# A two-layer encoder: the step sizes' projection in one block of 128 columns, and three transfers at other places

## The chip, the core and the metric

The kernel runs on one core of a Trainium2 chip. The metric is the device time of one execution in microseconds (us). The core has five engines that work through their own queues of instructions in order: TensorE (PE in the profile; PEld is its loading of weights), VectorE (DVE), ScalarE (ACT), GpSimd (POOL) and SyncE (SP, which here issues transfers only). They wait for each other through semaphores. Matmuls write to PSUM; everything else lies in SBUF or in the device's DRAM.

## The reference

512 tokens of 1024 channels go through two layers. Each layer is a token mixer and an ffn, each between two RMS norms and with a residual sum:

```
for layer in range(2):
    hn = rms_norm(x, norm_mix_pre[layer])
    m = retention_na_mixer(hn, ...) if layer == 0 else ssd_mixer(hn, ...)
    x = x + rms_norm(m, norm_mix_post[layer])
    f = conv_geglu_ffn(rms_norm(x, norm_ffn_pre[layer]), ...)
    x = x + rms_norm(f, norm_ffn_post[layer])
```

The change touches the second layer's mixer above all. It projects `hn` to gates z (2048 columns), inputs, B and C (3072), which go through a depthwise conv of width 5 and a silu, and raw step sizes (64 columns: 32 heads in two directions). From these come the step sizes and the decays of a chunked scan:

```
dt = softplus(dt_raw + dt_bias)
A = -exp(a_log)
log_a = dt * A
y = bidir_scan(C, B, x * dt[forward], x * dt[backward], log_a[forward], log_a[backward])
```

The scan works in chunks of 128 tokens: it needs cumulative sums of `log_a` in a chunk, and exponentials of these and of their differences to the chunk's total.

## The kernel before

**Precision.** Every fp32 product is made of three matmuls in a reduced fp32 type. A weight `w` is split by `split` (lines 84–87) into `hi`, a rounded copy (a CAST on ScalarE), and `lo`, what is left (a subtraction on VectorE); activations are split likewise into `xh` and `xl`. `mm3` adds hi·xh, lo·xh and hi·xl. In the profile these are lines L91, L92 and L93.

**Weights.** They come in units of 128 x 1024 (512 KB). `wunit` (lines 61–76) takes a tile `wst` (three buffers), issues the transfer on SyncE's queue, and splits it into `whi` and `wlo` (four buffers each) or into given tiles. A unit is one projection of 128 output columns: `proj_fm` runs 8 blocks of contraction x 3 matmuls of 512 tokens (24 matmuls), or in two token halves of 256 (48 smaller ones). The splits are given a priority of 60 over their place in the program, so that the scheduler may put them ahead.

**Order.** A scheduler takes the program's instructions in order of priority, with the tiles' buffers and dependencies as limits, and writes one fixed queue for each engine. An engine never passes an instruction that waits. `E.flush` runs the transposes of the last two token tiles (`LATE`), held back from the stage before so that projections may stand beside them.

**Start.** `trunk` issues the transfer of the first token tile, then that of the gain `g0` (a row broadcast to 128 partitions, 512 KB), then the other three token tiles, with the first weights between them. Each tile goes through `norm`: a sum of squares (ScalarE, Square, `sumsq` L128), a power -0.5 (GpSimd), a scaling `xs` (VectorE L139), transposes (TensorE L148) and the split into `xh` and `xl`. ScalarE loads a table of functions (ACT_TABLE_LOAD) where the function to come is not in the one loaded.

**Second mixer.** `mixer1` first projects three units (for the scan's `bf`, `cf` and the first `xf`) in two token halves: while the first half runs, the late token tiles are normed, transposed and split (lines 883–889). Then come the three convs: ScalarE opens each with scale and bias (L693), and VectorE adds four more taps (L696, two of 511 and two of 510 columns). Then `steps` (lines 597–665): the 64 columns of step sizes in 24 matmuls, `z` (L616), the softplus as a long chain on VectorE in `log1p_exp_neg` (L277 to L287, with one reciprocal), `dt`, `la`, the scan `pf` (L628), the totals `tot`, `et` and its diagonal matrix `diag` for a matmul `pe` that spreads the totals, the exponentials `ysc` and `sw`, a logarithm of `dt` (`lp_e`), and the transposes of `lp_e` and `sw` to tokens (`pt`, L664), copied to `tok`. Three more units for `xf` follow, their silus (L702, L705), and then the groups by an order written out by hand (`SLOTS`): the further projections `t6` to `t9` and those of the next group, the states, heads and pairs. The states need `sw`, the heads `lp_e` and `pf`.

**Mixer's end and last ffn.** The last group's output products run for each token tile with the two residual halves read back from `xd` (L869), each tile is normed, and the ffn (`ffn`, lines 223–270) starts with four units in token halves; the first two go to `whi` and `wlo`, the other two to tiles `hh` and `hl` of the ffn's own pool, which lies in memory that the mixer held.

Of the kernel before, what the change touches and what calls it, by code (L numbers as in the profile page):

```python
# [7 lines left out]
F32 = mybir.dt.float32  # L8
R32 = mybir.dt.float32r
BF16 = mybir.dt.bfloat16  # L10
U32 = mybir.dt.uint32
AF = mybir.ActivationFunctionType
ALU = mybir.AluOpType
# [13 lines left out]
class Env:  # L27
# [30 lines left out]
        self.xl = self.res.tile([P, KD, S], R32, name="xl")  # L58
        self.late, self.xs = [], {}

    def wunit(self, src, parts=None):


        nc = self.nc
        st = self.wst.tile([P, 1024], F32, name="wst")
        nc.sync.dma_start(st, src)
        halves = slice(0, 512), slice(512, 1024)
        if parts is None:
            hi, lo = self.whi.tile([P, 1024], R32, name="whi"), self.wlo.tile([P, 1024], R32, name="wlo")
            with self.tc.high_priority(60):  # L70
                self.split(hi, lo, st)
            return [(hi[:, c], lo[:, c]) for c in halves]
        with self.tc.high_priority(60):
            for j, c in enumerate(halves):
                self.split(parts[j], parts[j + 2], st[:, c])
        return [(parts[j], parts[j + 2]) for j in range(2)]

    def bcast(self, row):

        g = self.gain.tile([P, D], F32, name="gain")  # L80
        self.nc.sync.dma_start(g, row.partition_broadcast(P))
        return g

    def split(self, hi, lo, src):
# [135 lines left out]
    E.late += [lambda s=s: E.finish(s, st, done) for s in LATE]  # L220


def ffn(E, w_up, cw, w_down, g_post_row, done):

    nc, tc = E.nc, E.tc
    with ExitStack() as ctx:
        hp = ctx.enter_context(tc.tile_pool(name="ffn_h", bufs=NF))
        cp = ctx.enter_context(tc.tile_pool(name="ffn_c", bufs=1))
        cwt = cp.tile([P, 2, NF, 4], F32, name="cwt")
        nc.sync.dma_start(cwt, cw)  # L230
        hs = []

        def conv(ps, s, f):
            w = lambda i: cwt[:, s, f, i:i + 1]
            o = E.tmp.tile([P, S], F32, name=f"cv{s}", tag="tmp")
            nc.scalar.activation(o, ps, AF.Identity, scale=w(1), bias=w(3))  # L236
            nc.vector.scalar_tensor_tensor(o[:, 1:], ps[:, :S - 1], w(0), o[:, 1:], op0=ALU.mult, op1=ALU.add)  # L237
            nc.vector.scalar_tensor_tensor(o[:, :S - 1], ps[:, 1:], w(2), o[:, :S - 1], op0=ALU.mult, op1=ALU.add)  # L238
            return o

        def tail(f, pg, pv):
            g = conv(pg, 0, f)
            nc.scalar.activation(g, g, AF.Gelu_apprx_tanh)
            v = conv(pv, 1, f)
            nc.vector.tensor_tensor(v, g, v, op=ALU.mult)  # L245
            h = (hp.tile([P, S], R32, name="hh"), hp.tile([P, S], R32, name="hl"))
            E.split(*h, v)
            hs.append(h)

        extra = lambda i=0: [hp.tile([P, S], R32, name=n) for n in ("hh", "hh", "hl", "hl")]  # L250
        w0 = [[E.wunit(w_up[s, f], extra() if 2 * f + s >= 2 else None) for s in range(2)] for f in range(2)]
        p0 = [[E.mm.tile([P, S], F32, name="mm") for s in range(2)] for f in range(2)]
        for c in range(2):
            for i in range(4):
                f, s = i // 2, i % 2
                E.proj_fm(p0[f][s], w0[f][s], c * 256, c * 256 + 256)
                if c == 0 and i in (1, 2):
                    E.flush()
        for f in range(2):
            tail(f, *p0[f])  # L260
        for f in range(2, NF):
            ps = []
            for s in range(2):
                w = E.wunit(w_up[s, f])
                ps.append(E.mm.tile([P, S], F32, name="mm"))
                E.proj_fm(ps[-1], w)
            tail(f, *ps)
        g_post = E.bcast(g_post_row)
        batches = [[(0, u)] for u in (2, 2, 2, 2, 2, 1)] + [[(1, u)] for u in (2, 2, 1, 6)]
        down_tm(E, batches, w_down, lambda k: hs[k], g_post, done, lambda i: extra() if i not in (2, 3) else None)  # L270
# [289 lines left out]
TAIL = ("x0 s0", "x1 s1", "x2 s2 t0", "x3 s3 t1")  # L560


def mixer1(E, w_dt, w_fm, cw, dtc, cols, mask, w_out, g_post_row, done):

# [4 lines left out]
    with ExitStack() as ctx:  # L571
# [22 lines left out]
        pd = E.dram.tile([H2, S], F32, name="pd")  # L594
        yd = E.dram.tile([H2, S], F32, name="yd")

        def steps():

            st = E.wst.tile([P, 512], F32, name="wst")
            nc.sync.dma_start(st, w_dt)  # L600
            wh = E.whi.tile([P, 512], R32, name="whi")
            wl = E.wlo.tile([P, 512], R32, name="wlo")
            E.split(wh, wl, st)
            ps = E.mm.tile([P, S], F32, name="mm")
            for k in range(KD):
                c = slice(k * H2, k * H2 + H2)
                E.mm3(ps[:H2], wh[:, c], wl[:, c], E.xh[:, k], E.xl[:, k], k == 0, k == KD - 1)
            bc = few.tile([P, 3], F32, name="bc")
            nc.sync.dma_start(bc, dtc)
            nc.scalar.activation(bc[:, 1:2], bc[:, 1:2], AF.Exp)  # L610
# [4 lines left out]
            for i in range(2):  # L615
                nc.scalar.activation(z[i * H2:i * H2 + H2], ps[:H2, i * 256:i * 256 + 256], AF.Identity,  # L616
                                     bias=bc[:H2, 0:1])
            with tc.tile_pool(name="lp", bufs=1) as lpp:
                dt = lpp.tile([P, 256], F32, name="dt")
                sw = lpp.tile([P, 256], F32, name="sw")  # L620
# [227 lines left out]
        def out_mm(o, t, ws):  # L848
            ps = E.mm.tile([P, 512], F32, name="mm")
            tt = slice(t * P, (t + 1) * P)  # L850
            for k in range(4):
                yh, yl = o["y"][k]
                E.mm3(ps, yh[:, tt], yl[:, tt], *ws[k], k == 0, k == 3)
            return ps
# [26 lines left out]
            silus(o)  # L881

        w0 = [E.wunit(w_fm[0, i]) for i in range(3)]
        p0 = [E.mm.tile([P, S], F32, name="mm") for _ in range(3)]
        for c in range(2):
            for i, (w, ps) in enumerate(zip(w0, p0)):
                E.proj_fm(ps, w, c * 256, c * 256 + 256)
                if c == 0 and i > 0:
                    E.flush()
        for i in range(3):  # L890
            project(gs[0], i, p0[i])
        steps()
        three, ys, last = pool("m1e", 5), pool("m1y", 2), pool("m1f", 1)
        for _ in range(3):
            load(nc.sync)
# [32 lines left out]
        def fin(t, n, m):  # L928
# [2 lines left out]
        t4 = lambda pool, tags: [pool.tile([P, 512], R32, name="wo", tag=t) for t in tags]  # L931
        ws = [E.wunit(w_out[NG - 1, 0, 0]) + E.wunit(w_out[NG - 1, 0, 1]),
              E.wunit(w_out[NG - 1, 1, 0], t4(one, ("state00", "state10", "state01", "state11"))) + E.wunit(w_out[NG - 1, 1, 1], t4(four, ("yh", "yh", "yl", "yl")))]
        first = [out_mm(gs[-1], 0, ws[n]) for n in range(2)]
        rms(gs[-1])
        for t in range(NT):
# [6 lines left out]
def trunk(tc, x, norms, ab, ssd, ffns, out):  # L943

    nc = tc.nc
    with ExitStack() as ctx:
        E = Env(ctx, tc)
        w0 = []
        for t in range(NT):
            nc.sync.dma_start(E.x[:, t, :], x[t * P:(t + 1) * P])  # L950
            if t == 0:
                g0 = E.bcast(norms[0, 0])
            else:
                w0.append(E.wunit(ab[0][0, len(w0)]))
        for t in range(NT):
# [17 lines left out]

        mixer0(E, w0, *ab, norms[0, 1], then(norms[0, 2]))
        ffn(E, *ffns[0], norms[0, 3], then(norms[1, 0]))
        mixer1(E, *ssd, norms[1, 1], then(norms[1, 2]))
        ffn(E, *ffns[1], norms[1, 3], store)
        while E.late:
            E.flush()

# [106 lines left out]
```

## Time and profile before

| | us |
|---|---|
| three runs | 1420.84, 1422.07, 1422.39 (median 1422.07) |
| the profiled execution | 1422.91 |
| its span | 1421.1 |
| TensorE busy | 1395.8 (98%) |
| VectorE busy | 909.3 (64%) |
| ScalarE busy | 710.6 (50%) |
| GpSimd busy | 60.9 (4%) |

The profile is of one execution; its span is the time from the first to the last instruction, and 1.8 us lie around it. A matmul counts as busy from its start to its modelled end, and the next starts before that, so what a matmul costs in a row of matmuls is read from start to start. The clock granted to TensorE is given as a share of full speed (1.00 is 2.4 GHz, 0.50 is 1.2 GHz); on the page it is at 9 tenths or more in all forty slices.

### The profile page before, as it was taken

To read this page: it belongs to the slowest core of one execution; us is meant where nothing else is said; L and a number is where in the kernel's file an instruction comes from. 1 tells how busy PE (TensorE), PEld (TensorE's weight loads), DVE (VectorE), ACT (ScalarE), POOL (GpSimd) and SP (SyncE) were. 2 spreads that over 40 slices of the span, in tenths; PEclk is the share of its full clock that TensorE was granted. 3 is DMA by queue.
4 is the path that set the end of the run, shared out by engine and by line. 5 is a ranking of instruction groups with operands and counts; after the bars stand their busy time and mean duration, and the time that the engine had idled before them with its cause. 6 is when DMAs were issued, how large, how long until landed. Compare 5 with 4: busy or idle time off the path is not lost.

```text
span 1421.1 us, 17833 instructions
## 1 busy us (share of the span) xinstructions
PE 1395.8 (98%) x6838; PEld 1141.2 (80%) x6838; DVE 909.3 (64%) x1345; ACT 710.6 (50%) x1194; POOL 60.9 (4%) x66
## 2 busy tenths in 40 slices
PE   7999999999999999999999999999989999999998
PEld 6877777898888888888788788787878888888886
DVE  7368888765656652347878686997785665664232
ACT  5346666444444432324878787487344444443230
POOL 1010110100000000000000000010110000000000
PEclk9999999999999999999999999999999999999999
DMA  7443232233233322323566464363342233333231
GB/s 284 150 132 104 85 89 80 77 108 104 89 104 91 102 89 93 129 106 106 140 183 182 148 184 143 101 190 112 124 144 74 91 102 91 102 96 98 89 104 60
DMA packets 56437, 166.33 MB, mean 117 GB/s; under 512 B 6689, under 2 KB 7457, under 8 KB 56353
## 3 DMA queue, kind: packets, MB, share of 16 engines
q1 hardware_dynamic: 48464, 149.99, 33.2%
q10 hardware_dynamic: 7888, 15.21, 3.9%
q8 instruction: 54, 0.88, 0.3%
q14 instruction: 31, 0.25, 0.1%
HBM read 157.57 MB, written 5.51 MB: 115 GB/s over the span
## 4 chain that ended last, share of the span: by engine, by line
PE 89%; DVE 4%; ACT 3%; issue 2%; DMA 1%; POOL 0%; DVEq 0%; SPq 0%; POOLq 0%; ACTq 0%
PE mm L91 27%; PE mm L92 27%; PE mm L93 27%; PE pi L783 2%; PE py L803 1%; PE st L732 1%; PE y L459 1%; PE pt L148 1%; PE sc L443 1%; DVE wlo L87 1%; PE pt L676 0%; PE sc L444 0%; ACT whi L86 0%; DMA x<-in_x 0%; PE pt L511 0%
## 5 line engine op out<-in xcount | busy, mean ns | idle before, releaser
L91 PE MATMUL mm<-xh,whi 128*128 128x512 f32 (+1 forms) x1216 | 463.9, 382 | 0.4 <-ACT xh L86 0.2
L93 PE MATMUL mm<-xl,whi 128*128 128x512 f32 (+2 forms) x1216 | 463.3, 381 | 0.0
L92 PE MATMUL mm<-xh,wlo 128*128 128x512 f32 (+2 forms) x1216 | 462.1, 380 | 0.0
L87 DVE TENSOR_TENSOR wlo<-wst,whi 128x1024 fp32r<-128x1024 f32 (+1 forms) x208 | 254.8, 1226 | 135.0 <-ACT whi L86 131.7
L86 ACT CAST whi<-wst 128x1024 fp32r<-128x1024 f32 (+1 forms) x208 | 216.5, 1042 | 145.1 <-PE mm L92 123.4
L91 PEld LDWEIGHTS mm<-xh,whi 128*128 128x128 f32 x1216 | 228.3, 188 | 45.7 <-issue 2.3
L93 PEld LDWEIGHTS mm<-xl,whi 128*128 128x128 f32 (+1 forms) x1216 | 228.1, 188 | 44.1 <-issue 1.1
L92 PEld LDWEIGHTS mm<-xh,wlo 128*128 128x128 f32 (+1 forms) x1216 | 228.4, 188 | 42.4 <-issue 0.2
L237 DVE SCALAR_TENSOR_TENSOR cv<-mm,cwt,cv 128x511 f32<-128x511 f32 x88 | 66.0, 750 | 150.5 <-ACT cv L236 150.5
L236 ACT ACTIVATE cv<-mm,cwt 128x512 f32<-128x512 f32 x88 | 68.7, 780 | 128.0 <-PE mm L93 128.0
L91 PE MATMUL mm<-whi,hh 128*128 128x512 f32 x288 | 112.0, 389 | 0.0
L92 PE MATMUL mm<-whi,hl 128*128 128x512 f32 x288 | 112.0, 389 | 0.0
L93 PE MATMUL mm<-wlo,hh 128*128 128x512 f32 x288 | 112.0, 389 | 0.0
L762 ACT ACTIVATE pb<-pb,tok 128x128 f32<-128x128 f32 x256 | 81.3, 391 | 5.7 <-DMA pb<-pd 3.2
L86 ACT CAST hh<-cv 128x512 fp32r<-128x512 f32 x44 | 27.3, 621 | 103.3 <-DVE cv L245 103.3
L238 DVE SCALAR_TENSOR_TENSOR cv<-mm,cwt,cv 128x511 f32<-128x511 f32 x88 | 66.0, 750 | 3.0
L93 PEld LDWEIGHTS mm<-wlo,hh 128*128 128x128 f32 x288 | 54.1, 188 | 11.3
L91 PEld LDWEIGHTS mm<-whi,hh 128*128 128x128 f32 x288 | 54.1, 188 | 11.2
L92 PEld LDWEIGHTS mm<-whi,hl 128*128 128x128 f32 x288 | 54.1, 188 | 11.2
L696 DVE SCALAR_TENSOR_TENSOR xf<-mm,cwt,xf 128x511 f32<-128x511 f32 (+1 forms) x64 | 47.5, 744 | 8.1 <-ACT xf L693 7.8
L87 DVE TENSOR_TENSOR hl<-cv,hh 128x512 fp32r<-128x512 f32 x44 | 30.5, 693 | 28.9 <-ACT hh L86 28.9
L128 ACT ACTIVATE junk<-mm 128x512 bf16<-128x512 f32 x24 | 14.3, 596 | 68.7 <-PE mm L93 68.6
(250 smaller groups left out, 1877.1 us busy)
## 6 DMA issues: line engine op xcount, KB each, us to landing
wst<-in_f_up SPq DMA_DIRECT2D x88, 512.0 KB
wst<-in_f_down SPq DMA_DIRECT2D x44, 512.0 KB
wst<-in_c_fm SPq DMA_DIRECT2D x40, 512.0 KB
pb<-pd ACTq DMA_DIRECT2D x29, 512.0 KB
wst<-in_ab_fm SPq DMA_DIRECT2D x20, 512.0 KB
gain<-yd SPq DMA_DIRECT2D x32, 256.0 KB
wst<-in_c_out SPq DMA_DIRECT2D x16, 512.0 KB
gain<-in_norms SPq DMA_DIRECT2D x8, 512.0 KB
```

Of the source, the lines that this page charges most:

```text
L86: self.nc.scalar.copy(hi, src)
L87: self.nc.vector.tensor_tensor(lo, src, hi.bitcast(F32), op=ALU.subtract)
L91: mm(out, lh, rh, start=first, stop=False)
L92: mm(out, ll, rh, start=False, stop=False)
L93: mm(out, lh, rl, start=False, stop=last)
L128: self.nc.scalar.activation(self.junk[:, :w], src, AF.Square, scale=float(n) ** -0.5, accum_out=s)
L236: nc.scalar.activation(o, ps, AF.Identity, scale=w(1), bias=w(3))
L237: nc.vector.scalar_tensor_tensor(o[:, 1:], ps[:, :S - 1], w(0), o[:, 1:], op0=ALU.mult, op1=ALU.add)
L238: nc.vector.scalar_tensor_tensor(o[:, :S - 1], ps[:, 1:], w(2), o[:, :S - 1], op0=ALU.mult, op1=ALU.add)
L696: nc.vector.scalar_tensor_tensor(r[:, a], ps[:, b], wc(j), r[:, a], op0=ALU.mult, op1=ALU.add)
L762: nc.scalar.activation(pb[:, dr, c], pb[:, dr, c], AF.Identity, scale=1.0 - 2 * dr, bias=tok[:, 0, c, dr * H + h:dr * H + h + 1])
L783: nc.tensor.matmul(pi[:, c - 1 + dr], o["st"][dr, i][:, q * P:(q + 1) * P], o["t"][1][:, c * C:(c + 1) * C], start=True, stop=True)
```

## The change

1. **Steps' projection.** The weights' `hi` and `lo` parts stand side by side in one tile, for each of 8 blocks 64 + 64 columns. One matmul of 128 columns gives both parts' products in two halves of the partitions; with `xh` and `xl`, in two token halves of 256, these are 2 x 8 x 2 = 32 matmuls (`steps_proj`; the product lo·xl, left out before, is now in it). Two additions on VectorE join the parts into `z`. The projection and the whole chain behind it stand between the two token halves of the first three units, no longer behind their convs.
2. **Start.** The gain's transfer is issued by ScalarE. ScalarE runs one tiny Square of a constant before it waits for the first token tile, so that the table load belongs to that.
3. **Last ffn.** Its first two units and the transfer of the third are asked for within mixer1 (`ahead`), before the last group's first output products, and the transfer of the conv weights `cwt` after the four units.

```diff
+    def wload(self, src):
+        st = self.wst.tile([P, 1024], F32, name="wst")
+        self.nc.sync.dma_start(st, src)
+        return st
...
-    def bcast(self, row):
+    def bcast(self, row, eng=None):
         g = self.gain.tile([P, D], F32, name="gain")
-        self.nc.sync.dma_start(g, row.partition_broadcast(P))
+        (eng or self.nc.sync).dma_start(g, row.partition_broadcast(P))
...
-        nc.sync.dma_start(cwt, cw)
...
-        w0 = [[E.wunit(w_up[s, f], extra() if 2 * f + s >= 2 else None) for s in range(2)] for f in range(2)]
+        u0, u1, st = w1 or (E.wunit(w_up[0, 0]), E.wunit(w_up[1, 0]), None)
+        w0 = [[u0, u1], [E.wunit(w_up[0, 1], extra(), st), E.wunit(w_up[1, 1], extra())]]
+        nc.sync.dma_start(cwt, cw)
...
-        def steps():
+        def steps_weights():
             st = E.wst.tile([P, 512], F32, name="wst")
             nc.sync.dma_start(st, w_dt)
-            wh = E.whi.tile([P, 512], R32, name="whi")
-            wl = E.wlo.tile([P, 512], R32, name="wlo")
-            E.split(wh, wl, st)
-            ps = E.mm.tile([P, S], F32, name="mm")
+            w = E.whi.tile([P, KD, 2, H2], R32, name="whi")
+            with tc.high_priority(60):
+                E.split(w[:, :, 0], w[:, :, 1], st.rearrange("p (k h) -> p k h", k=KD))
+            return w.rearrange("p k a h -> p k (a h)")
+
+        def steps_proj(ps, w, c):
+            cc = slice(c * 256, c * 256 + 256)
             for k in range(KD):
-                c = slice(k * H2, k * H2 + H2)
-                E.mm3(ps[:H2], wh[:, c], wl[:, c], E.xh[:, k], E.xl[:, k], k == 0, k == KD - 1)
+                for j, x in enumerate((E.xh, E.xl)):
+                    nc.tensor.matmul(ps[:, cc], w[:, k], x[:, k, cc], start=k + j == 0, stop=k + j == KD)
+
+        def steps(ps):
...
+                nc.vector.tensor_tensor(z[i * H2:i * H2 + H2], ps[H2:, i * 256:i * 256 + 256], z[i * H2:i * H2 + H2], op=ALU.add)
...
-        p0 = [E.mm.tile([P, S], F32, name="mm") for _ in range(3)]
+        wd = steps_weights()
+        p0 = [E.mm.tile([P, S], F32, name="mm") for _ in range(4)]
         for c in range(2):
-            for i, (w, ps) in enumerate(zip(w0, p0)):
-                E.proj_fm(ps, w, c * 256, c * 256 + 256)
+            if c == 1:
+                steps_proj(p0[3], wd, 0)
+                steps_proj(p0[3], wd, 1)
+                steps(p0[3])
+            for i, w in enumerate(w0):
+                E.proj_fm(p0[i], w, c * 256, c * 256 + 256)
...
         for i in range(3):
             project(gs[0], i, p0[i])
-        steps()
...
+        ahead()
         first = [out_mm(gs[-1], 0, ws[n]) for n in range(2)]
...
-                g0 = E.bcast(norms[0, 0])
+                g0 = E.bcast(norms[0, 0], nc.scalar)
+                nc.scalar.activation(E.junk[:, :1], E.mhalf, AF.Square)
...
+        def ahead():
+            up = ffns[1][0]
+            w1.extend((E.wunit(up[0, 0]), E.wunit(up[1, 0]), E.wload(up[0, 1])))
```

Line numbers move with the change: the split is L86 and L87 before, L92 and L93 after; the convs' taps L696 before, L713 after.

**VectorE's order at mixer1's beginning.** The first piece is of before, with the splits of the fifth, sixth and seventh projections' weights (`wlo_5559`, `wlo_5596`, `wlo_5680`; the first three projections are those in token halves):

```order
L87 TENSOR_TENSOR wlo_5559<-wst_5556,whi_5558 128x1024
L696 SCALAR_TENSOR_TENSOR xf_5356<-mm_5171,cwt_5134,xf_5356 128x510
L277 SCALAR_TENSOR_TENSOR lp_e_5410<-z_5397 128x256
L87 TENSOR_TENSOR wlo_5596<-wst_5593,whi_5595 128x1024
L279 TENSOR_SCALAR lp_s_5411<-lp_e_5410 128x256
L87 TENSOR_TENSOR wlo_5680<-wst_5677,whi_5679 128x1024
L280 RECIPROCAL lp_s_5411<-lp_s_5411 128x256
L281 TENSOR_TENSOR lp_s_5411<-lp_s_5411,lp_e_5410 128x256
```

The second is of after, where `wlo_5690` is the seventh projection's:

```order
L713 SCALAR_TENSOR_TENSOR xf_5597<-mm_5572,cwt_5135,xf_5597 128x511
L642 TENSOR_SCALAR la_5316<-dt_5326,bc_5311 128x256
L643 MEMSET msk_5329 128x256
L675 TENSOR_SCALAR lp_e_5387<-dt_5326 128x256
L644 MEMSET msk_5329 128x2
L713 SCALAR_TENSOR_TENSOR xf_5597<-mm_5572,cwt_5135,xf_5597 128x510
L645 SCALAR_TENSOR_TENSOR pf_5317<-msk_5329,la_5316 128x256
L713 SCALAR_TENSOR_TENSOR xf_5597<-mm_5572,cwt_5135,xf_5597 128x510
L649 COPY tot_5361<-pf_5317 128x2
L93 TENSOR_TENSOR wlo_5690<-wst_5687,whi_5689 128x1024
L652 TENSOR_TENSOR pf_5317<-pf_5317,la_5316 32x256 x2
```

The seventh projection's split stood between the first operations of the softplus, ahead of the reciprocal and of all taps of the fourth projection's conv (`xf_5526` of before). Now it stands behind the whole softplus, the scan `pf`, the totals `tot` and the fifth projection's taps (`xf_5597` of after).

**ScalarE's order at the same place.** First before, from the table load for the logarithm on:

```order
L659 ACT_TABLE_LOAD
L659 ACTIVATE lp_e<-lp_e 128x256
L651 ACT_TABLE_LOAD
L651 ACTIVATE ysc<-pf 32x256
L638 ACTIVATE et<-tot 128x2
L651 ACTIVATE ysc<-pf 32x256
L86 CAST whi<-wst 128x1024
L654 ACTIVATE sw<-pf 32x256 x2
L652 ACTIVATE ysc<-tm 32x256
L653 ACTIVATE sw<-tm 32x256
L652 ACTIVATE ysc<-tm 32x256
```

And after, from the same load on (L668 to L671 are the exponentials, L722 a silu):

```order
L676 ACT_TABLE_LOAD
L676 ACTIVATE lp_e<-lp_e 128x256
L655 ACT_TABLE_LOAD
L655 ACTIVATE et<-tot 128x2
L668 ACTIVATE ysc<-pf 32x256 x2
L722 ACT_TABLE_LOAD
L722 ACTIVATE xf<-xf 128x512
L669 ACT_TABLE_LOAD
L669 ACTIVATE ysc<-tm 32x256
L663 COPY etot<-pe 128x2x2x64
L670 ACTIVATE sw<-tm 32x256
```

A silu of the first `xf` now stands between the exponentials, with a table load ahead of it and one behind it; a weights' cast that stood there has moved behind them, and `et` has moved ahead of the first `ysc`.

**SyncE's order around the last ffn.** First before (`wst<-in_f_up` is an up-projection unit's transfer, `x<-xd` the residual's):

```order
L66 DMA wst<-in_f_up 128x1024
L81 DMA gain<-in_norms 128x1024
L66 DMA wst<-in_f_up 128x1024 x2
L81 DMA gain<-in_norms 128x1024
L66 DMA wst<-in_f_up 128x1024 x2
L869 DMA x<-xd 128x512 x8
L66 DMA wst<-in_f_up 128x1024
```

And after:

```order
L64 DMA wst<-in_f_up 128x1024
L87 DMA gain<-in_norms 128x1024
L64 DMA wst<-in_f_up 128x1024 x2
L87 DMA gain<-in_norms 128x1024
L64 DMA wst<-in_f_up 128x1024 x2
L886 DMA x<-xd 128x512 x8
L64 DMA wst<-in_f_up 128x1024
```

The five up-projection transfers stand at the same places relative to the gains and to the residual's transfers, and the conv weights' transfer follows in both orders behind these rows.

At the start, ScalarE's queue of after begins with the gain's transfer, the table load and the tiny Square; then two sums of squares, the first weights' cast and the third sum of squares stand ahead of the first cast of `xh`, where before only two sums and the weights' cast stood ahead of it.

## Rows read from the trace of the kernel before

**Rows 1.** Windows: stretch, us, busy (instructions) of PE, PEld, DVE, ACT, POOL, clock, DMA share, GB/s.

```profile
0.00:14.00 14.00, 5.30 (x20) 4.05 (x20) 6.22 (x13) 8.07 (x12) 2.37 (x9) 1.00 0.88 322
...
660.00:690.00 30.00, 30.00 (x148) 24.19 (x147) 29.22 (x55) 17.33 (x23) 0.00 (x0) 1.00 0.27 88
690.00:712.00 22.00, 21.17 (x101) 14.99 (x100) 16.80 (x28) 20.04 (x49) 0.00 (x0) 1.00 0.82 206
712.00:1012.00 300.00, 299.04 (x1573) 242.41 (x1573) 240.03 (x354) 216.79 (x437) 18.53 (x13) 1.00 0.52 153
```

**Rows 2.** Waits of PE: what waited for what, us in total, times, longest.

```profile
PE pt L148 <- DVE xs L139: 9.1, 4, 8.2
PE mm L91 <- ACT hh L86: 3.9, 2, 3.2
```

**Rows 3.** Timeline of PE, mixer1's beginning: start us, us, instruction, [idle before it].

```profile
654.40 0.39 PE L91 MATMUL mm<-xh,whi 128*128 128x256 f32 x1 [0.24 <-ACT xh L86]
654.63 0.28 PE L92 MATMUL mm<-xh,wlo 128*128 128x256 f32 x1
654.75 0.29 PE L91 MATMUL mm<-xh,whi 128*128 128x256 f32 x1
...
663.35 0.39 PE L92 MATMUL mm<-xh,wlo 128*64 128x512 f32 x1
...
668.41 0.39 PE L93 MATMUL mm<-xl,whi 128*64 128x512 f32 x1
668.64 0.39 PE L91 MATMUL mm<-xh,whi 128*128 128x512 f32 x1
...
670.00 0.39 PE L91 MATMUL mm<-xh,whi 128*128 128x512 f32 x1
```

**Rows 4.** Timeline of DVE in mixer1, 668 to 700.

```profile
671.50 1.22 DVE L87 TENSOR_TENSOR wlo<-wst,whi 128x1024 fp32r<-128x1024 f32 x1
672.64 1.74 DVE L280 RECIPROCAL lp_s<-lp_s 128x256 f32<-128x256 f32 x1
...
677.61 0.41 DVE L285 TENSOR_TENSOR lp_r<-lp_r,lp_q 128x256 f32<-128x256 f32 x1
677.94 0.74 DVE L696 SCALAR_TENSOR_TENSOR xf<-mm,cwt,xf 128x510 f32<-128x510 f32 x1
678.60 0.28 DVE L286 TENSOR_SCALAR lp_r<-lp_r 128x256 f32<-128x256 f32 x1
678.80 1.22 DVE L87 TENSOR_TENSOR wlo<-wst,whi 128x1024 fp32r<-128x1024 f32 x1
679.94 0.42 DVE L285 TENSOR_TENSOR lp_r<-lp_r,lp_q 128x256 f32<-128x256 f32 x1
```

**Rows 5.** Timeline of ACT in mixer1, 655 to 700.

```profile
658.28 0.78 ACT L693 ACTIVATE bf<-mm,cwt 128x512 f32<-128x512 f32 x1 [3.44 <-PE mm L93]
...
681.64 0.61 ACT L705 ACTIVATE xf<-xf 128x512 f32<-128x512 f32 x1
...
688.62 1.28 ACT L651 ACT_TABLE_LOAD   x1
689.91 0.42 ACT L651 ACTIVATE ysc<-pf 32x256 f32<-32x256 f32 x1
```

**Rows 6.** Timeline of ACT at the start, 3 to 13.

```profile
4.25 1.28 ACT L128 ACT_TABLE_LOAD   x1 [4.25 <-DMA x<-in_x]
...
10.01 0.58 ACT L86 CAST xh<-pt 128x512 fp32r<-128x512 f32 x1
10.49 1.06 ACT L128 ACTIVATE junk<-x 128x1025 bf16<-128x1025 f32 x1
```

**Rows 7.** Timeline of PE at the start, 3 to 13.

```profile
11.24 0.77 PE L91 MATMUL mm<-whi,xh 128*128 128x512 f32 x1
```

**Rows 8.** Windows of 2 us at the last ffn's beginning, columns as in rows 1.

```profile
1056.00:1058.00 2.00, 1.54 (x5) 1.30 (x6) 2.00 (x4) 1.98 (x4) 0.00 (x0) 0.50 0.33 86
...
1062.00:1064.00 2.00, 2.00 (x17) 2.00 (x16) 0.43 (x1) 1.05 (x2) 0.00 (x0) 0.85 0.32 129
```

More of the change, by code (lines that the diff above doesn't have):

```diff
@@ L59, in __init__, with wunit @@
         self.late, self.xs = [], {}
-    def wunit(self, src, parts=None):
-        nc = self.nc
+    def wload(self, src):
         st = self.wst.tile([P, 1024], F32, name="wst")
-        nc.sync.dma_start(st, src)
+        self.nc.sync.dma_start(st, src)
+        return st
+    def wunit(self, src, parts=None, st=None):
+        if st is None:
+            st = self.wload(src)
         halves = slice(0, 512), slice(512, 1024)
@@ L220, in down_tm, with ffn @@
     E.late += [lambda s=s: E.finish(s, st, done) for s in LATE]
-def ffn(E, w_up, cw, w_down, g_post_row, done):
+def ffn(E, w_up, cw, w_down, g_post_row, done, w1=None):
     nc, tc = E.nc, E.tc
@@ L560, with mixer1 @@
 TAIL = ("x0 s0", "x1 s1", "x2 s2 t0", "x3 s3 t1")
-def mixer1(E, w_dt, w_fm, cw, dtc, cols, mask, w_out, g_post_row, done):
+def mixer1(E, w_dt, w_fm, cw, dtc, cols, mask, w_out, g_post_row, done, ahead):
     nc, tc = E.nc, E.tc
@@ L975, in trunk @@
         ffn(E, *ffns[0], norms[0, 3], then(norms[1, 0]))
-        mixer1(E, *ssd, norms[1, 1], then(norms[1, 2]))
-        ffn(E, *ffns[1], norms[1, 3], store)
+        w1 = []
+        def ahead():
+            up = ffns[1][0]
+            w1.extend((E.wunit(up[0, 0]), E.wunit(up[1, 0]), E.wload(up[0, 1])))
+        mixer1(E, *ssd, norms[1, 1], then(norms[1, 2]), ahead)
+        ffn(E, *ffns[1], norms[1, 3], store, w1)
         while E.late:
```

## Prediction

> **What bounds the kernel now.** I read the windows table first, then the waits of TensorE, then the timelines of the places that the change touches. The windows table shows TensorE busy in nearly all of every long stretch: 299.04 of 300 us in 712–1012, all 30 of 660–690 [rows 1]. So time can be gained or lost only where TensorE stops, where its matmuls cost something, and where its clock is low. The waits name two large stops: 9.1 us on the first `xs` (8.2 of them the start) and 3.9 us on the casts `hh` at the last ffn's beginning [rows 2]. In mixer1's beginning, where most of the change lies, TensorE hardly waits, but VectorE is nearly as full: 29.22 of 30 us in 660–690, and in 690–712 ScalarE is the fullest but one, with 20.04 of 22 [rows 1]. A change there is a matter of who is late, not of how much work there is.
>
> **Steps' matmuls.** Before, 24 products of 64 weight columns with 512 tokens; the run of 23 starts at 663.35, the last at 668.41, and the next projection at 668.64: 5.29 us, 0.23 each; one more stands alone among the earlier ones, 5.5 us in all [rows 3]. After, 2 halves x 8 blocks x 2 inputs = 32 products of 128 columns with 256 tokens. Such a product starts 0.12 after the one before it (654.63, 654.75) [rows 3], so 32 x 0.12 = 3.84. They stand ahead of the matmul at 654.40 that waited 0.24 for a cast of `xh` [rows 3], and cover that wait: counted from 654.16, they end at 658.0, the 72 second-half products of the first three projections (72 x 0.12 = 8.64) at 666.6, where before they and the steps ended at 668.6. **−2.0**. The two additions of the weight parts (64x256 on VectorE) have no row; the nearest are a 128x256 product at 0.33 start to start and a conv part of 511 columns at 0.66 [rows 4]. I take 0.4 each, between the two. They lie ahead of the conv parts, while VectorE waits for the first projection, and cost the path nothing as long as it does.
>
> **What the moved chain does to VectorE.** The orders of before and after decide this term. I number the projections of 512 columns by their place: the fourth starts at 668.64 before. Before, VectorE splits the fifth to seventh projections' weights (`wlo`) ahead of the reciprocal: the seventh's starts at 671.50, and TensorE needs it some 13 us later (668.64 + 3 x 24 x 0.227 = 685.0, with 0.227 from 668.64 to 670.00, six products) [rows 3, 4]. After, the chain of the step sizes begins ahead of the conv parts, and each of its links stands between two of them; the seventh's `wlo` stands behind the scan and the copy `tot`. Summing VectorE's list in the after order from the first conv part to the end of that `wlo`, start to start from [rows 4]: 20 conv parts x 0.66 = 13.2; 3 `wlo` x 1.14 = 3.4; the reciprocal 1.74; 10 two-input operations of 128x256 x 0.33 = 3.3; 10 with one input x 0.20 = 2.0; scan, memsets and copy about 1 (an estimate: the scan as two of those with one input, the others smaller). 24.6 us. The list can start when the first projection has ended (658.0 + 24 x 0.12 = 660.9) and ScalarE has opened its conv (0.78) [rows 5]: 661.7. The seventh's `wlo` ends at **686.3**.
>
> TensorE meanwhile: the fourth projection 666.6 to 672.1; the fifth's `wlo` ends at 672.7 by the same list, two products are put before it, a wait of 0.2; fifth and sixth end at 683.1. The order has three products with `whi` alone (seventh, eighth, ninth) before the first that reads the late `wlo`; these end at 683.8. Then TensorE stands until 686.3: **+2.5, with the small wait +2.7**. Bounds: nothing if VectorE's list is 10% shorter than summed, +4 if it loses a microsecond to links that wait for each other.
>
> **What it does to ScalarE.** Before, the loads of the function tables near there are Silu, Ln, Exp, all exponentials, Silu. After, a Silu load, one silu and another Exp load stand between the first exponentials and those that make `sw`. A load takes 1.28 (the activation behind it starts 1.29 later), an exponential 0.42, a silu 0.61 [rows 5]. By VectorE's list the fourth projection's convs end at 680.6; Silu load, three silus, Ln load, Ln, Exp load: 680.6 + 1.28 + 1.8 + 1.28 + 0.42 + 1.28 = 686.7, where `et` runs, not later than the `tot` that it needs. From there: two exponentials 0.84, Silu load 1.28, silu 0.61, Exp load 1.28, an exponential, the copy of `etot` (taken as a silu) and five exponentials 3.1, `sw`'s product on VectorE 0.33: 694.1. TensorE, after 686.3, does 7 products (688.0), `pe` and the first transposes of `lp_e` (to 688.7), 16 products (3.6): it comes to `sw`'s transposes at 692.3 and waits **1.8**. What before lost in 690–712 (22 − 21.17 = 0.8 [rows 1]) is at these places and is replaced: **−0.8**. Bounds 0 to +2.5. Queued behind ScalarE's late exponentials are the copies of `tok`, then the heads' first exponentials; TensorE doesn't come to these before it has 26 more products to do.
>
> The Trainium skill (ScalarE: Activation LUTs, section What ACT_TABLE_LOAD costs) adds a drain of about 1380 ns to a load of 1283 ns, for every switch to another set. By that the two loads added would cost 5.3 instead of 2.6, `sw` would be 2.8 later, and the sum 2.8 higher. The load's length agrees with the row; the drain does not show, since 1.29 lies between the load's start and that of its activation [rows 5]. The sum goes by the row.
>
> Mixer1: −2.0 + 2.7 + 1.8 − 0.8 = **+1.7**. Nothing after it gives this back: in 712–1012 TensorE waits 0.96 us in all [rows 1].
>
> **Start.** ScalarE's table load stood behind the first x until 4.25, and now runs ahead: up to 1.28 off the first norm [rows 6]. The gain's transfer of 512 KB moves from the second place of SyncE's queue to ScalarE's own, to be issued beside the first x. The bytes ahead of the third x are the same, so what waits for that lands as before. And in the order of after, the third sum of squares stands ahead of the first cast of `xh`: before, the cast ran at 10.01 and the sum at 10.49, as soon as its x was there [rows 6]. Now the cast can start at 10.49 + 1.06 = 11.55, 1.5 later, and TensorE's first projection matmul (11.24 before [rows 7]) needs it. From −1.3 (the table's load and nothing lost) to +1.5; I take **+0.9**, nearer to the loss, since a queue in order can't pass the waiting sum, and some of it is made up where the next tiles' casts no longer have a sum between them.
>
> A rule of the Trainium skill (DMA: Bandwidth & Descriptors, section Issuing engines are not separate DMA queues) says that transfers issued by several engines run on the same 16 engines and interleave, so only the issue is saved. By it the first x lands later than before, and the table's 1.28 is mostly eaten; no row of before shows two queues at once.
>
> **Last ffn.** The change asks for two up-projection units and a third's transfer before mixer1's last output products. In the orders of both kernels, SyncE's queue has the five up-projection loads at the same places ahead of the loads from `xd`, and the `hh` casts have the same four kinds of waits, since their tiles lie in memory that mixer1 frees last. So the 3.9 us of [rows 2] and the half clock behind them stay: **0** (−6.5 to +0.5). That this part of the change does nothing is thus part of the forecast.
>
> **Sum.** +1.7 + 0.9 + 0 = **+2.6** in a profiled execution of 1422.91 (span 1421.1), which stands 0.8 over the median of 1422.07. On the median: **1424.7**. A measurement of this kernel can tell some 0.2% (2.8 us) from no change; the forecast lies just inside that.
>
> **Rivals.**
> 1. *VectorE keeps up.* If the list takes 22 us or less, the seventh `wlo` is there at 683.8 and only the saved matmuls and part of the `sw` wait remain: −2.0 + 0.9 + 0 to 0.9, about −0.5, 1421.5; with nothing lost at the start either, 1419. For it: before, the same operations interleave without idle time. Against: the sum has no slack in it, and the start to start figures are from that very stretch.
> 2. *The early load works.* Then the 3.9 us go [rows 2], and the low clock behind the stop: 0.50 in three windows of 2 us and 0.85 in a fourth [rows 8], 3.0 + 0.3 us. 2.6 − 7.2: 1417.5. Against: the order there has not moved. For: only waits on semaphores are the same, not when they come.
> 3. *The new stop lowers the clock.* A mechanism with one place: TensorE idle from 683.8 to 686.3. At 1052–1056 it stopped for 3.2 and then 0.7 us, and ran at 0.50 (1.2 GHz) after it [rows 2, 8]. If 2.5 us suffice, the 3.3 us of rival 2 are added here: +5.9, 1428. It decides from a stop somewhere between the 0.8 us of short waits in 690–712, where the clock stayed at 1.00 [rows 1], and that one. The Trainium skill (TensorE: Matmul & The Clock Gate, section Why this matters for your kernels) also warns that idle gaps between bursts bring the half rate back; the row agrees for the longer gap.
> 4. *The start gains.* −1.3 instead of +0.9: 1422.5.
>
> **Chances.** Forecast 0.45 (half on each side of the bound: 0.23 same, 0.22 slower), rival 1 0.20 (0.14 same, 0.06 faster), rival 2 0.10 (faster), rival 3 0.13 (slower), rival 4 0.12 (0.08 same, 0.04 faster where the sums of mixer1 come low too). Faster 0.20, same 0.45, slower 0.35. The range, 1418.4 to 1428.6, takes in rivals 1, 3 and 4 and leaves out rival 2 and the ends of the bounds.
>
> **What would show it.** The steps as 32 products of about 3.8 us before 658.5, and a projection of 512 columns starting near 666.6. TensorE idle some 2.5 us on the seventh projection's `wlo` near 684–686, and near 692 on `sw`, with two table loads more on ScalarE. The first projection matmul near 12, not 11. At the last ffn the same 3.2 and 0.7 us and 0.50 of the clock. It is wrong if mixer1's stretch has no idle time beyond 1 us, if the stop on `hh` shrinks, or if the first projection matmul comes ahead of 11.

## The result, and the profile after

| | before | after |
|---|---|---|
| median, us | 1421.45 (4 runs) | 1429.15 (4 runs, 1428.31 to 1429.49) |
| ratio | | 1.0046, 95% interval 1.0033 to 1.0059 |
| profiled execution, its span | 1422.91, 1421.1 | 1429.12, 1427.3 |

The change makes the kernel slower, by 6.5 us (4.7 to 8.4) by the ratio; the two medians differ by 7.7. The forecast was +2.6, to 1424.7, with a range to 1428.6. The median measured, 1429.15, lies just above that range; the ratio put on the forecast's own median before, 1422.07, gives 1428.6, its very end.

To see where, I follow three marks through both traces: the last transposes before mixer1's second token half (653.13 before, 654.40 after), the last `pg` matmuls in the fourth group (965.21, 972.00), and the transposes within the last ffn's beginning (1062.06, 1068.56). TensorE is 1.3 us late at the first mark, 6.8 at the second and 6.5 at the third. So in these two traces the start costs 1.3, mixer1 5.5, and the last ffn nothing.

The windows of after, around mixer1's beginning (columns as in rows 1):

```profile
654.00:690.00 36.00, 33.40 (x199) 28.79 (x197) 29.99 (x60) 19.05 (x27) 0.00 (x0) 1.00 0.17 54
690.00:712.00 22.00, 17.83 (x86) 13.40 (x87) 12.38 (x19) 19.32 (x38) 0.00 (x0) 1.00 0.77 196
```

TensorE, full in 660–690 before [rows 1], now stands 2.6 us in the first and 4.2 in the second; the clock stays at 1.00. The timeline of TensorE there:

```profile
667.74 0.40 PE L97 MATMUL mm<-xh,whi 128*128 128x512 f32 x1
...
673.20 0.61 PE L97 MATMUL mm<-xh,whi 128*128 128x512 f32 x2
673.90 0.50 PE L98 MATMUL mm<-xh,wlo 128*128 128x512 f32 x1
...
684.50 0.61 PE L97 MATMUL mm<-xh,whi 128*128 128x512 f32 x2
686.45 0.47 PE L97 MATMUL mm<-xh,whi 128*128 128x512 f32 x1 [1.33 <-DVE tot L649]
687.56 0.50 PE L98 MATMUL mm<-xh,wlo 128*128 128x512 f32 x1 [0.64 <-DVE wlo L93]
...
689.06 0.40 PE L98 MATMUL mm<-xh,wlo 128*128 128x512 f32 x1
690.03 0.70 PE L661 MATMUL pe<-diag,ones 128*128 128x256 f32 x2 [0.57 <-DVE diag L659]
...
694.22 0.39 PE L99 MATMUL mm<-xl,whi 128*128 128x512 f32 x1
696.80 0.44 PE L681 MATMUL pt<-head,sw 128*128 128x128 f32 x2 [2.19 <-DVE sw L673]
...
704.10 0.39 PE L97 MATMUL mm<-xh,whi 128*128 128x512 f32 x1
706.43 1.09 PE L693 MATMUL pt<-head,xf 128*128 128x128 f32 x8 [1.95 <-ACT xf L722]
```

What a stop costs is read from start to start: a product of 512 columns comes 0.227 after the one before in a row without stops. From 684.73 (the second of the pair at 684.50) to 689.06 are 8 products, 1.8 us of work in 4.33: 2.5 lost. `pe` comes 0.97 after the last of them, 0.7 too late; the transposes of `sw` come 2.58 after the last product, 2.3 too late; those of `xf` 2.33, 2.1 too late. **7.7 us** in all, where the bracketed idle times sum to 6.7: idle time is counted from the modelled end of the product before, 0.39 after its start, while the next one is due after 0.227. For the same reason one small stop shows no bracket: the first `wlo` product of the fifth projection starts at 673.90 and not at 673.65, 0.2 late. The fourth projection starts at 667.74, where before it was 668.64 [rows 3] with a mark 1.27 earlier: the block of 128 columns saved 2.2 us.

The splits of the fifth and of the seventh projection's weights on VectorE, and the copy `tot`:

```profile
672.63 1.22 DVE L93 TENSOR_TENSOR wlo<-wst,whi 128x1024 fp32r<-128x1024 f32 x1
...
686.22 0.16 DVE L649 COPY tot<-pf 128x2 f32<-128x2 f32 x1
686.29 1.22 DVE L93 TENSOR_TENSOR wlo<-wst,whi 128x1024 fp32r<-128x1024 f32 x1
```

The last two stops are ScalarE's:

```profile
688.92 0.20 ACT L655 ACTIVATE et<-tot 128x2 f32<-128x2 f32 x1
689.03 0.82 ACT L668 ACTIVATE ysc<-pf 32x256 f32<-32x256 f32 x2
689.86 1.28 ACT L722 ACT_TABLE_LOAD   x1
691.15 0.63 ACT L722 ACTIVATE xf<-xf 128x512 f32<-128x512 f32 x1
691.80 1.28 ACT L669 ACT_TABLE_LOAD   x1
693.10 0.42 ACT L669 ACTIVATE ysc<-tm 32x256 f32<-32x256 f32 x1
...
703.53 0.40 ACT L779 ACTIVATE pb<-pb,tok 128x128 f32<-128x128 f32 x1 [2.43 <-DMA pb<-pd]
703.94 1.28 ACT L719 ACT_TABLE_LOAD   x1
705.23 0.63 ACT L719 ACTIVATE xf<-xf 128x512 f32<-128x512 f32 x1
705.77 0.61 ACT L722 ACTIVATE xf<-xf 128x512 f32<-128x512 f32 x1
```

Two loads and a silu stand between `et` and the exponentials for `sw`, as the order said. And one activation of the first head waits 2.43 for the transfer of `pb`, with the silus that TensorE needs queued behind it. Before, the head's first activation also ran at 703.53, but the silus stood ahead of it, and the transfer is issued less than 1 us later than before (697.52, before 696.58). So what costs is the place of the silus behind the wait; a run below with the silus ahead loses this stop.

The start, ScalarE and then TensorE:

```profile
1.17 1.28 ACT L976 ACT_TABLE_LOAD   x1 [1.17 <-PEq L1107]
...
6.17 1.06 ACT L134 ACTIVATE junk<-x 128x1025 bf16<-128x1025 f32 x1 [3.50 <-DMA x<-in_x]
...
10.09 1.06 ACT L134 ACTIVATE junk<-x 128x1025 bf16<-128x1025 f32 x1 [0.24 <-DMA x<-in_x]
...
11.15 0.56 ACT L92 CAST xh<-pt 128x512 fp32r<-128x512 f32 x1
```

```profile
11.77 0.80 PE L97 MATMUL mm<-whi,xh 128*128 128x512 f32 x1 [1.85 <-ACT xh L92]
```

The table is there early, but the first x lands only near 6.1 (4.25 before [rows 6]), so its sum of squares starts 0.6 later than before (4.25 and a load of 1.29 made 5.54); and the cast of `xh` runs after the third sum, 1.14 later than before. TensorE's first projection matmul starts 0.5 later (11.24 before [rows 7]).

At the last ffn, the waits of TensorE keep their place and size, 3.10 and 0.46, and the half clock behind them stays:

```profile
1062.26 0.58 PE L97 MATMUL mm<-xh,hh 128*128 128x256 f32 x1 [3.10 <-ACT hh L92]
1063.30 0.58 PE L97 MATMUL mm<-xh,hh 128*128 128x256 f32 x1 [0.46 <-ACT hh L92]
```

### The profile page after: what moved, and what is told of

Its sections match the earlier page's. It is cut to its first block, busy times and chain, and to the rows that moved or that the text cites. A ratio compares the mean times of both kernels' runs of the same rounds, so it can differ in the third digit from the quotient of the medians.

```text
span 1427.3 us, 17860 instructions
## 1 busy us (share of the span) xinstructions
PE 1394.7 (98%) x6846; PEld 1141.0 (80%) x6846; DVE 909.7 (64%) x1347; ACT 713.7 (50%) x1197; POOL 63.2 (4%) x66
## 4 chain that ended last, share of the span: by engine, by line
PE 88%; DVE 5%; ACT 4%; issue 1%; DMA 1%; POOL 1%; SPq 0%; DVEq 0%; POOLq 0%; ACTq 0%
PE mm L97 26%; PE mm L98 26%; PE mm L99 26%; PE st L749 1%; PE pi L800 1%; PE py L820 1%; PE y L467 1%; PE pt L154 1%; PE pt L693 1%; DMA x<-in_x 1%; DVE xf L713 1%; PE sc L451 1%; DVE wlo L93 0%; PE sc L452 0%; DMA pb<-pd 0%
## 5 line engine op out<-in xcount | busy, mean ns | idle before, releaser
L99 PE MATMUL mm<-xl,whi 128*128 128x512 f32 (+1 forms) x1208 | 460.7, 381 | 0.0
L98 PE MATMUL mm<-xh,wlo 128*128 128x512 f32 (+1 forms) x1208 | 459.6, 381 | 0.7 <-DVE wlo L93 0.6
L93 DVE TENSOR_TENSOR wlo<-wst,whi 128x1024 fp32r<-128x1024 f32 x207 | 253.4, 1225 | 138.1 <-ACT whi L92 136.3
L92 ACT CAST whi<-wst 128x1024 fp32r<-128x1024 f32 (+1 forms) x208 | 216.7, 1042 | 153.4 <-PE mm L98 125.4
L99 PEld LDWEIGHTS mm<-xl,whi 128*128 128x128 f32 x1208 | 227.2, 188 | 44.0 <-issue 1.4
L98 PEld LDWEIGHTS mm<-xh,wlo 128*128 128x128 f32 x1208 | 227.3, 188 | 43.1 <-DVE wlo L93 1.5
L92 ACT CAST hh<-cv 128x512 fp32r<-128x512 f32 x44 | 27.3, 621 | 103.4 <-DVE cv L251 103.4
L713 DVE SCALAR_TENSOR_TENSOR xf<-mm,cwt,xf 128x511 f32<-128x511 f32 (+1 forms) x64 | 47.6, 747 | 7.9 <-ACT xf L710 7.5
L93 DVE TENSOR_TENSOR hl<-cv,hh 128x512 fp32r<-128x512 f32 x44 | 30.5, 693 | 28.9 <-ACT hh L92 28.9
```

Source lines behind the costliest of these rows:

```text
L92: self.nc.scalar.copy(hi, src)
L93: self.nc.vector.tensor_tensor(lo, src, hi.bitcast(F32), op=ALU.subtract)
L98: mm(out, ll, rh, start=False, stop=False)
L99: mm(out, lh, rl, start=False, stop=last)
L713: nc.vector.scalar_tensor_tensor(r[:, a], ps[:, b], wc(j), r[:, a], op0=ALU.mult, op1=ALU.add)
```

## Experiments

Ratios are to the kernel before on the same chip, with 95% intervals. "Mixer1's passage" is the time from the first to the second mark above: 312.1 us before, 317.6 after. In four traces of kernels that leave mixer1 as it is (the start alone twice, the table load alone, the early units alone), it is 311.2 to 312.0, so less than 1 us says nothing.

**The parts alone.** The start:

```diff
-                g0 = E.bcast(norms[0, 0])
+                g0 = E.bcast(norms[0, 0], nc.scalar)
+                nc.scalar.activation(E.junk[:, :1], E.mhalf, AF.Square)
```

> The kernel before with the start alone: the gain's transfer on ScalarE's queue and the tiny Square. Theory (the first x lands later because two transfers now run side by side): TensorE's first transposes near 8.8 instead of 8.17, the second layer's mixer reached 1.3 us later as in the changed kernel, +1.0 to +1.5 us in all. Rival (the start's shift is made up by slack before mixer1, the whole loss is mixer1's): within 0.4 us of before.

Measured 1.0026 (1.0014 to 1.0039), +3.7 us, above both theory and rival, though mixer1 was reached only 0.9 us late in the trace, the first transposes at 8.76. The trace is of the shortest of its 12 executions (1421.6; nine of the others took over 1425). So I ran it again:

> The start alone once more, for a second trace: in the first, mixer1 was reached 0.9 us late and the end came no later, while most of its executions took some 4 us more than that one. Theory (the delay at the start moves the layer's early transfers and GpSimd's rotation against each other, and TensorE stops near 88 us on rk, as in two other traces): the median again +3 to +5 us, and the trace of a longer execution shows 1.5 us or more of idle time at 86 to 92 us, or a lower clock behind it. Rival (the first trace is typical and the longer times were the chip's): the median within 1.5 us of before.

Measured 1.0019 (1.0009 to 1.0029): executions from 1421.3 to 1428.6, and the trace once more of the shortest. Slower it is, by +2.7: less than the theory's +3 to +5, more than the rival's 1.5. The theory on where the longer executions lose could not be read, and stays open. A stop on `rk`, the first mixer's rotated keys, near 88 us does come and go: it is 2.4 us in a trace whose start is that of before (below) and 0.45 in these two. The first mark lies at 653.7 to 655.3 in the five traces with the changed start (the latest with a stop on `rk` of 1.6), and in the nine with the gain in SyncE's queue at 652.5 to 653.5, but for two at 657.0, both with a stop on `rk` of over 1.6: on the whole the start's 1 to 2 us are there, within a spread of that size.

The same Square, with the gain left in SyncE's queue:

> The kernel before with the tiny Square alone; the gain stays second in SyncE's queue. Theory (the queue is what costs): the first x lands near 4.25 as before, its sum of squares starts there and not 1.28 later, the first transposes come about 0.8 earlier since they then wait for the gain; -0.8 to 0 us in all. Rival (running the table load early by itself puts the order of casts and sums wrong and costs): +0.5 or more.

1.0005 (0.9996 to 1.0014): no difference. The first x's sum started at 4.43 and the first transposes at 7.31, 0.9 earlier, but the next ones and the first projection matmul ran as before (10.47, 11.23): they wait for later transfers. In the order of this kernel the cast of `xh` again stands ahead of the third sum. So the early load alone is neutral, and the start's loss comes with the gain's other queue. The other queue without the early load was not run.

Mixer1's part, and the last ffn's early units, each with its lines of the change's diff and no others:

> The kernel before with mixer1's part alone (merged block and the chain moved ahead of the convs). Theory: the stops on the late weight split, on the diagonal, on the scaled steps and on the silu stay as in the changed kernel: +4.5 to +5.7 us. Rival (the start's delay and the early ffn transfers take part in it): under +3.

1.0050 (1.0032 to 1.0068), +7.1. Passage 317.6; the same five stops (1.37, 0.64, 0.68, 2.20, 1.98).

> The kernel before with the last ffn's early units alone. Theory (the scheduler had already put these transfers there, so nothing moves): within 0.3 us of before, the stop on hh 3.0 to 3.3 us and a second one of 0.4 to 0.7. Rival (the transfers come earlier though their place is the same): the stop shrinks and 1 us or more is gained.

1.0005 (0.9996 to 1.0013); stops 3.11 and 0.65. Nothing moved.

**Block or place.** The block behind the convs; the old products at the early place; the block early with the chain behind the convs:

```diff
         for i in range(3):
             project(gs[0], i, p0[i])
-        steps()
+        wd, psd = steps_weights(), E.mm.tile([P, S], F32, name="mm")
+        steps_proj(psd, wd, 0)
+        steps_proj(psd, wd, 1)
+        steps(psd)
```

> The kernel before with the merged block of 128 columns, but projection and chain left behind the first three projections' convs. Theory (the block itself is a gain, its place is the loss): 32 x 0.12 in place of 5.5 us of matmuls, no new stop: -1.2 to -1.9 us. Rival (the block costs, by the two additions that the chain waits for or by its fourth product): 0 or slower.

1.0037 (1.0024 to 1.0049), +5.3, passage 318.4: the theory failed. The block's matmuls ran as meant, but the scheduler gave the other engines another order. On VectorE three splits stand ahead of `dt`, and `tot` comes at 694.78 (689.65 before); on ScalarE the logarithm stands behind all exponentials. The waits of TensorE from 654 to 730 are two new ones:

```profile
PE mm L97 <- ACT z L719: 3.2, 1, 3.2
PE pt L681 <- DVE lp_e L677: 2.5, 1, 2.5
```

Behind both, the clock fell: the window from 704 to 708, behind `lp_e`, ran at 0.58, and the one from 724 to 728, behind `z`, at 0.57. So this run tests a different order and not the old place by itself; what the block would cost or save there is not shown, and so the rival's cause is not, though its number came.

```diff
+            if c == 1:
+                steps_proj(p0[3], wd)
+                steps(p0[3])
```

> The kernel before with projection and chain moved to the early place, but with the old 24 products of 64 columns. Theory (the place is the loss): the stops of the mixer-alone kernel stay and the 1.7 us saved in matmuls are missing: +6 to +9 us. Rival (the block and its additions make the loss): under +3.

1.0048 (1.0034 to 1.0062), +6.8; passage 318.2. Stops on splits (1.2 in two), on `lp_e` (1.5) and on `sw` (2.2), and a clock of 0.83 and 0.75 in the two windows from 696 to 704. So the early place loses without the block too.

```diff
                 steps_proj(p0[3], wd, 1)
-                steps(p0[3])
...
             project(gs[0], i, p0[i])
+        steps(p0[3])
```

> The kernel before with the merged block at the early place, but the chain of the step sizes left in the program behind the first three projections' convs. Theory (the chain's place in VectorE's and ScalarE's queues is the loss, the block's matmuls are a gain): no stop on the late weight split, on the scaled steps or on the silu beyond 0.6 us; -1.5 to -2.5 us. Rival (the early matmuls, their PSUM tile or the weights' split ahead of others make the loss): +2 or more.

Passage 310.0, 2.1 less than before, with one wait from 654 to 730, 0.6 on a split. The time was 0.9996 (0.9987 to 1.0005), with executions from 1418.55 to 1425.17; the shortest is 2.1 under the shortest of before (1420.66 in 15). In its own trace TensorE stopped near 88 us, in a part that this kernel does not touch, and the clock fell behind it:

```profile
90.44 0.79 PE L451 MATMUL sc<-rq,rk 128*128 128x512 f32 x1 [2.40 <-DVE rk L385]
```

```profile
88.00:92.00 4.00, 1.60 (x5) 1.23 (x5) 3.87 (x6) 3.37 (x5) 0.00 (x0) 0.78 0.32 69
92.00:96.00 4.00, 4.00 (x17) 3.06 (x15) 3.84 (x9) 3.75 (x5) 0.00 (x0) 0.80 0.15 62
```

It reached mixer1 at 657.0. Thus such a stop can eat the gain in an execution. The measurement itself shows no gain: the passage is shorter, the time the same.

The same line moved in the changed kernel itself, beside the changed kernel:

> The changed kernel with one line moved: the chain of the step sizes stands behind the first three projections' convs again, the block's matmuls stay early. Theory (the chain's place is mixer1's whole loss): mixer1 is passed in 2.1 us less than before instead of 5.5 more, so 6.5 to 8 us faster than the changed kernel and within 2 us of before. Rival (part of the loss comes from the start or the early ffn units): less than 5 us faster than the changed kernel.

> The changed kernel itself beside the others on one chip. Theory: mixer1's part +5.5 and the start +1 to +1.3, +6 to +8 us. Rival (the parts do not add up, since the late start was given back in mixer1 in the start's own trace): +4.5 to +6.

The changed kernel: 1.0063 (1.0049 to 1.0077), +9.0 by the ratio; the medians differ by 7.5. By the medians that is within the theory's +6 to +8, by the ratio above it; the passage is 316.9 in this trace. With the chain late: 1.0011 (1.0002 to 1.0019), passage 309.8; 6.9 us under the changed kernel by the medians (1422.63 against 1429.56), as the theory had it. That one line is mixer1's whole loss, and what is left of the block is a passage 2.2 shorter than before (1.4 shorter than the shortest of the four with mixer1 as it was). As mixer1 (+5.5) and the start (+1 to +4) add to what the whole measures within their intervals, no third part is needed.

**Which queue.** In the mixer-alone kernel, the silus ahead:

```diff
-            silus(o)
+            with tc.high_priority(100) if 5 in ii else nullcontext():
+                silus(o)
```

> The mixer-alone kernel with the silus of the first group's fifth and sixth projections given a higher priority: in ScalarE's queue no silu and no two table loads stand between the exponentials any more, and these silus stand ahead of the first head's activations that wait for a transfer. Theory (2.35 us are lost to the two table loads ahead of the scaled steps, 2.1 us to the silu behind the head's wait): both stops fall under 0.6, the stops on the late weight split and the diagonal (together 3.1 us) stay; 3.5 to 4.5 us faster than mixer alone, +2 to +3.5 us on before. Rival (the loss is VectorE's alone, ScalarE's order only shows where it is paid): the gain on mixer alone is under 1.5.

1.0033 (1.0021 to 1.0046), +4.7: 2.4 us less than mixer alone, each by its own ratio, between theory and rival; the two intervals overlap, and the passage of 316.8 is only 0.8 shorter. The stop on the silu was gone, and a new one of 3.02 came at 724.67, on the silus of `z`, again behind an activation of a head that waits for a transfer; behind it the window from 724 to 728 ran at a clock of 0.57. The two loads were gone too, and `sw` came 1.8 earlier after the first mark; but the stop on it was still 1.85, since TensorE also came earlier. The stop on the late split, which the theory let stay, was gone: the scheduler now had the seventh projection's split ahead of `dt`,

```profile
680.69 1.22 DVE L93 TENSOR_TENSOR wlo<-wst,whi 128x1024 fp32r<-128x1024 f32 x1
681.83 0.42 DVE L641 SCALAR_TENSOR_TENSOR dt<-z,lp_r 128x256 f32<-128x256 f32 x1
```

so this run changed VectorE's order with ScalarE's and does not tell the two apart. TensorE's waits:

```profile
689.46 0.70 PE L661 MATMUL pe<-diag,ones 128*128 128x256 f32 x2 [0.44 <-DVE diag L659]
...
693.85 0.44 PE L681 MATMUL pt<-head,sw 128*128 128x128 f32 x2 [1.85 <-DVE sw L673]
...
724.67 0.79 PE L97 MATMUL mm<-xh,whi 128*128 128x512 f32 x1 [3.02 <-ACT z L719]
```

At last, the block early, the chain late, and the splits of the next projections' weights 40 further ahead (`wunit` takes its priority from `ahead_by`, 60 elsewhere):

```diff
+        E.ahead_by = 100
         tiles(gs[0], 3)
         tiles(gs[0], 4, 5)
+        E.ahead_by = 60
```

> The kernel with the block early and the chain late, and the weights' splits of the first group's fourth to sixth projections 40 further ahead in priority. Theory (a late split is the last stop left there, 0.59): that stop goes, mixer1 is passed in 2.5 us less than before, -2 to -3 us in all. Rival (what the splits gain, the chain loses: the scaled steps or lp_e come later and stop TensorE): no faster than the kernel without it, and a stop on sw or lp_e of 0.5 us or more.

1.0014 (1.0006 to 1.0023), passage 314.4: the rival held. The stop on the split went; in its place came 1.5 on the scaled inputs `xs`, 1.1 on `sw`, 0.8 on `z` and 0.7 on a head's `e`.

No version was measurably faster than before; the block early with the chain late is the nearest to it.

## Why the forecast was right in direction and too small

- **Steps' matmuls**, −2.0: 2.2 saved. Right.
- **The late split**, +2.7: 2.5 and 0.4 more at the fifth projection. The list came out as summed. The seventh `wlo` ran from 686.29, 1.2 us behind the summed start of 685.1 (686.3 less 1.14), because mixer1 itself came 1.27 later. TensorE lost 2.5 there. One detail differs: of the three products put before it, the third waited first (1.33). The profile names `tot`; I take it for a wait on the PSUM tile whose last taps end beside `tot`, just ahead of the split, which no run tests. The 0.2 at the fifth's split came as summed, after two products (from 673.20 to 674.24 three products took 1.04 and not 0.68). Beyond the sum, 0.7 on `pe` came, since `et` ran at 688.92 and not at 686.7. Of these 2.2 us, 1.3 are the later start; the rest is a weights' cast of 1.05 that stood ahead of the Silu load, where I let that load follow the fourth projection's taps at once.
- **`sw`**, +1.8: 2.3. The late `sw` and the two loads in its chain are as forecast. What the loads alone cost is not shown: without them `sw` came 1.8 earlier, but in an order where TensorE came earlier too and still stood 1.85.
- **What before lost there**, −0.8: its stops cost 0.4 on `sw` and `pe`, and 0.5 on `pi` (idle time), 0.9 together. Right for this trace; but the stop on `pi` comes and goes, and stands in two of the five traces that leave mixer1 as it is.
- **The step that failed**: "TensorE doesn't come to these before it has 26 more products to do". TensorE came after these 26 products, to the transposes of `xf`, and stood 2.1 us. What I had priced at nothing was not the head's activations but what is queued behind them: one of them waits for a transfer, and two silus wait with it. This term, 2.1, is the largest of the way from +1.7 to the measured +5.5 in mixer1. With 0.7 on `pe`, 0.5 more on `sw` and 0.2 more at the splits, less 0.2 more saved by the block and 0.1 by what before lost, that gives 4.9; about 0.6 is not assigned.
- **Start**, +0.9: 1.3 in the trace, by the mechanism told (the cast behind the third sum, and a first x that lands later), of which 0.5 is there at the first projection matmul. The chip's times of the start alone are higher, +2.7 and +3.7, and that difference is open.
- **Last ffn**, 0: right, in order, stops and time.
- **Rivals.** VectorE did not keep up; the last ffn's early load did nothing; the start did not gain. The new stops did not lower the clock in the trace of after, but in that of the same kernel run again they did: after the same 2.19 on `sw`,

```profile
696.00:700.00 4.00, 2.28 (x12) 2.28 (x13) 1.95 (x4) 3.92 (x9) 0.00 (x0) 0.76 0.47 138
700.00:704.00 4.00, 4.00 (x18) 3.35 (x17) 3.65 (x4) 2.68 (x6) 0.00 (x0) 0.82 0.76 207
```

 and there the stop on `xf` was missing, since TensorE came later. So rival 3 is right for some executions in its kind, not in its place or price: the fall came behind `sw` and not behind the late split, and what the two windows lack of the full clock, 0.24 and 0.18 of 4 us, is at most 1.7 us of work, where rival 3 has 3.3. There it took the place of the silu's stop.
- **Luck.** The range reaches to 1428.6 to take in rival 3, the clock (1428). In the trace of after the clock does not fall in mixer1, and what brought the time to that end is the stop on `xf`, which no rival has. That the range nearly held the result is luck; the direction is not.

## What to carry to other kernels

Before moving a chain ahead, write down for each in-order queue what then stands behind its links, and follow that to who needs it, also where the link itself is not urgent: a wait for a transfer (2.43 us here) holds everything behind it. Five arrangements of the same 32 matmuls and the same chain passed one stage in 309.8 to 318.4 us (some with a fall of the clock in it), a spread of four times the 2.2 that the block saves. Where two queues are nearly full, price the order that comes out, not the work saved, and undo one line at a time to find the one that counts.

## What was not expected of the hardware

- Two transfers of 512 KB issued side by side by two engines: the first x's reader started at 6.17 and 6.13 in two kernels, against 4.25 and 4.43 where the gain stood behind it in one queue. That agrees with the Trainium skill (DMA: Bandwidth & Descriptors, section Issuing engines are not separate DMA queues), by which transfers started by several engines run on the same 16 DMA engines and interleave. The urgent one paid 1.7 to 1.9 us for the other's own queue.
- After the same stop of 2.19 us TensorE's clock stayed at 1.00 in one execution, and in another of the same kernel it stood at 0.76 from 696 to 700. A stop's price is thus not one number, and the prediction's bracket for the stop that lowers the clock, between 0.8 and 3.2 us, has no one limit inside it.
- A table load of 1.28 was followed by its activation 1.29 or 1.30 after its start wherever that waited for nothing else, also with two loads close behind each other (689.86 to 691.15, 691.80 to 693.10). The Trainium skill (ScalarE: Activation LUTs, section What ACT_TABLE_LOAD costs) adds a drain of about 1380 ns to each switch; no row here shows it.
